# A streaming-encoder layer: branch gates and branch products with tokens on partitions

## The chip, the cores and the metric
The kernel runs on one core of one Trainium2 chip. The metric is the device time of one execution in microseconds (us), as the median of several runs. The core has a matmul engine (TensorE, PE in the profile; its weight loads are listed apart as PEld), VectorE (DVE), ScalarE (ACT), GpSimd (POOL) and SyncE (SP, which here only issues the loads of weights).

## The reference
One layer, 256 tokens, width 2048, float32:

```python
h = rms_norm(x, norm_mix_g)
z = h @ w_in    # qkv 3072 | a 8 | b 8 | gate 1024 | u, v 2048 | attention q, k, v 3072 | gate logits 3 x 2048
branch_a = gated_delta_net(qkv, a, b, gate) @ w_out_a       # 8 heads of 128, the inner width is 1024
u, vb = split(gelu(uv));  vb = layer_norm(vb)
s = einsum('gts,bnsgc->bntgc', ws, vb) + b_spatial          # blocks of 128 tokens, 8 groups
branch_b = (u * s) @ w_out_b
branch_c = stick_breaking_attention(q, k, v) @ w_out_c      # 8 heads of 128
gates = sigmoid(gate_logits)                                # [tokens, 3, 2048]
y = gates[0] * branch_a + gates[1] * branch_b + gates[2] * branch_c
x = x + y @ w_out
x = x + square(relu(rms_norm(x, norm_mlp_g) @ w_ff1)) @ w_ff2   # inner width 8192
```

## The kernel before
**Products in three matmuls.** To reach float32 accuracy, every operand is split into an exact high and low part (`hi` by a copy on ScalarE, `lo` by a subtraction on VectorE, in `split_w`, L151), and a product is the sum of hi x hi, hi x lo and lo x hi. The activations are kept split, as [128, k, 2, 256 tokens] (`actT` holds `hT`, the normalized input, and later `yT`; `aT`, `bT`, `cT` are the branches' inputs). Weights stream in: a `raw` tile of 1 MB (three buffers), which is four *pieces* of 128 x 512 numbers. Both forms of product work piece by piece; a piece is 128 inputs x 512 columns of weights, or 256 inputs x 256 columns, for all 256 tokens:

- `gemm_T` (L193) gives the product transposed, columns on partitions. The weights are stationary; the activations move. For each 128 x 128 block of weights one matmul moves 512 columns (both halves of the activations against `hi`) and one moves 256 (the high half against `lo`): 8 matmuls in a piece. In the trace these are `g<-hT,hi` (512) and `g<-hT,lo` (256), the moving tile first.
- `gemm` (L158) gives the product with tokens on partitions. The activations are stationary and 512 columns of weights move: for each of the two token tiles hi, lo, hi, which are 6 matmuls in a piece, in the trace `g<-hi,hT` and `g<-lo,hT`.

In `gemm_T` the right half of the sum stands in other columns of PSUM, so its reader adds two halves (`add_halves`, L223: a ScalarE copy and a VectorE addition).

**Order of work.** The matmul engine runs in program order; the other engines' order is laid out by a scheduler. `push` (L139) holds the matmuls of a piece back until 4 later pieces have been split (`LA = 4`). Work that is not a streamed product (DeltaNet, normalizations, attention, spatial mixing) consists of generators in the queue `side`; after each piece `pump(1)` runs the first of them to its next `yield`. So between two pieces there may be one step of background work, and `rest(n)` leaves n pieces free so that the other engines can finish what the next step needs.

**Stages.** Decay, gate and qkv projections with DeltaNet behind them (0 to 239 us); the gates of column group 0 (`gate_block(0, br)`, L814) as filling work behind the second DeltaNet half; v, then u of the spatial gating (L885 to L904); attention projections (L1030 to L1032); the gates of group 1 (L1037) as filling behind the attention; the gates of groups 2 and 3 (L1080); the branches' products (`branch_group`, L1046); the output projection; the MLP in four quarters. A column group is 512 of the 2048 columns. All gates and branch products use `gemm_T`, two calls of 256 columns for a group, so `y` is made transposed, as the output projection wants it. A gate's blocks are put into a [128, 4, 256] tile with `scaled_T` (two halves added, times 1 / rms along the free axis) and go through the sigmoid at once or, for groups 0 and 1, later in `early_gates`. At the first block of v, `open_mid` (L822) drains the background queue, releases DeltaNet's tiles and loads the spatial weights `wsT` and `bsp`; the mixing (`gmlp_mix`, L857) is put into the queue when the last block of u is done.

Of the kernel before, what the change touches and what calls it, by code (L numbers as in the profile page):

```python
# [9 lines left out]
F32 = mybir.dt.float32  # L10
# [10 lines left out]
def tile_hybrid_trunk(  # L21
# [48 lines left out]
    # ------------------------------------------------ background work queue  # L70
# [22 lines left out]
    # ------------------------------------------------ constants  # L93
# [7 lines left out]
    # the tensor engine is clocked up only under work: give it some while the first loads run  # L101
# [16 lines left out]
    def split_T(dst, k0, nk, pt, scale=None):  # L118
        """dst[:, k0:k0+nk] = the exact high and low parts of the (scaled) psum tile pt [P, nk, 256]"""
# [14 lines left out]
    # ------------------------------------------------ streamed products  # L134
    # Weights are split into exact high and low parts LA pieces ahead of the products that use them.
# [22 lines left out]
    def gemm(lhs, w, b, done, before=None, rate=0):  # L158
        """done([psum of token tile t]) gets act times block b of w, tokens on partitions"""
# [33 lines left out]
    def gemm_T(act, w, b, done, g0=0, ng=None, rate=0):  # L193
        """done([psum of 128 columns each]) gets (act times block b of w)^T, its low-part half on the right"""
# [71 lines left out]
    W_AG = (352, 344, 344)  # L266
    sgp_ctx = ExitStack()
# [9 lines left out]
    def row_norms():  # L277
        """1 / rms of x's rows, along the free axis (rb) and on partitions (r1); then they scale the first product"""
# [41 lines left out]
    # ------------------------------------------------ more constants  # L320
# [19 lines left out]
    # ------------------------------------------------ branch inputs, transposed  # L340
# [4 lines left out]
    # ================================================ gated DeltaNet  # L345
    gt0ctx = ExitStack()
    gtp0 = gt0ctx.enter_context(tc.tile_pool(name="gtp0", bufs=3))
# [3 lines left out]
    # lvl[b][s, c] = 1 where s lies in the first and c in the second half of one 2b block, in 64 x 64 blocks  # L351
# [26 lines left out]
    # scratch for moving the 16 x 16 diagonal blocks of a 64 x 64 block onto partitions of their own and back  # L378
# [27 lines left out]
    def gates_ab():  # L406
# [10 lines left out]
        # log1p(e) = 2 artanh(e / (2 + e))  # L417
# [32 lines left out]
    def conv_silu(zt, cb0, dst):  # L450
        """causal convolution along the free axis, and SiLU; zt [P, 4, T] is scaled by the row norms first"""
# [18 lines left out]
    def gdn_half(hf, tiles):  # L470
        """heads 4 hf .. 4 hf + 3, in chunks of 128, as tiles come in"""
# [25 lines left out]
        # decay[s, c] = exp(g_c - g_s) for s <= c  # L497
# [70 lines left out]
        # T = (I + L)^-1 and U = T^T: 16 x 16 blocks by substitution, then doubled to 128  # L568
# [76 lines left out]
        for b in (16, 32):  # L645
# [5 lines left out]
            # the last level takes T's first block only  # L651
# [24 lines left out]
        # u = T (beta v); w^T = (beta e^g k)^T T^T for the second chunk  # L676
# [14 lines left out]
        # the state after the first chunk, and what the second takes from it  # L691
# [16 lines left out]
        # output: o = e^g q S + intra v_new, normalized and gated  # L708
# [42 lines left out]
    def scaled_T(pt, dst):  # L751
        """dst = pt's sum of halves times the rows' 1 / rms"""
        add_halves(dst, pt)
        tt(dst, dst, rb, ALU.mult)

    def gate_block(j, br, pool, rate=0):
        gt = []

        def done(i):
            def f(ps):  # L760
                if i == 0:
# [489 lines left out]
```

## Time and profile before

| | us |
|---|---|
| median of 3 runs (lowest, highest) | 1724.08 (1722.41, 1724.3) |
| span of the profiled execution, first to last instruction | 1722.3 |
| matmul engine busy | 1697.8 |
| VectorE busy | 1186.4 |
| ScalarE busy | 963.9 |
| GpSimd busy | 169.5 |

No time of the profiled execution beside its span is shown; the span is 1.8 us below the median and 0.1 us below the lowest run. Busy time of the matmul engine counts a matmul from its issue to its modelled end, and the next one starts earlier than that; its pace is read from the distance of the starts, not from durations.

### The profile page before, as it was taken

To read this page: it belongs to the slowest core of one execution; us is meant where nothing else is said; L and a number is where in the kernel's file an instruction comes from. 1 tells how busy PE (TensorE), PEld (TensorE's weight loads), DVE (VectorE), ACT (ScalarE), POOL (GpSimd) and SP (SyncE) were. 2 spreads that over 40 slices of the span, in tenths; PEclk is the share of its full clock that TensorE was granted. 3 is DMA by queue.
4 is the path that set the end of the run, shared out by engine and by line. 5 is a ranking of instruction groups with operands and counts; after the bars stand their busy time and mean duration, and the time that the engine had idled before them with its cause. 6 is when DMAs were issued, how large, how long until landed. Compare 5 with 4: busy or idle time off the path is not lost.

```text
span 1722.3 us, 26815 instructions
## 1 busy us (share of the span) xinstructions
PE 1697.8 (99%) x9880; PEld 1480.8 (86%) x9880; DVE 1186.4 (69%) x2174; ACT 963.9 (56%) x1741; POOL 169.5 (10%) x225
## 2 busy tenths in 40 slices
PE   8998999999999999999999999999999999999999
PEld 7887888888888888888888888888888888888887
DVE  8885688466658666666787777666776677567764
ACT  5774576465567665555555555544554455445543
POOL 7134024000001000001222100000000000000000
PEclk9999999999999999999999999999999999999999
DMA  7445355355444455555556555555555555555563
GB/s 244 180 144 166 107 179 190 114 189 193 173 170 172 154 189 178 189 191 177 179 209 226 194 196 186 185 192 196 187 186 190 196 192 182 191 194 191 183 217 119
DMA packets 48211, 313.77 MB, mean 182 GB/s; under 512 B 5600, under 2 KB 7792, under 8 KB 12240
## 3 DMA queue, kind: packets, MB, share of 16 engines
q1 hardware_dynamic: 46224, 306.41, 51.2%
q0 software_dynamic: 1856, 5.65, 1.1%
q8 instruction: 77, 1.26, 0.3%
q14 instruction: 54, 0.44, 0.1%
HBM read 308.62 MB, written 3.42 MB: 181 GB/s over the span
## 4 chain that ended last, share of the span: by engine, by line
PE 90%; DVE 3%; DMA 3%; POOL 2%; issue 1%; ACT 1%; DVEq 0%; POOLq 0%; ACTq 0%
PE g L62 86%; PE pm L62 3%; DVE lo L65 1%; POOL tb L65 1%; POOL pr L65 1%; DMA Tm<-scrT 1%; DMA scrU<-ub 1%; DMA lb<-scrL 1%; DMA scrL<-LT 1%; ACT hi L154 0%; DVE qkT L65 0%; DMA ab_bc<-in_a_dt_dram 0%; ACT hT L239 0%; PE pm L928 0%; DVE qkT L458 0%
## 5 line engine op out<-in xcount | busy, mean ns | idle before, releaser
L65 DVE TENSOR_TENSOR lo<-raw,hi 128x512 fp32r<-128x512 f32 (+2 forms) x1168 | 815.3, 705 | 474.5 <-ACT hi L154 469.6
L154 ACT CAST hi<-raw 128x512 fp32r<-128x512 f32 (+2 forms) x1168 | 708.9, 615 | 613.6 <-PE g L62 559.6
L62 PE MATMUL g<-hT,hi 128*128 128x512 f32 x1280 | 464.1, 405 | 0.0
L62 PE MATMUL g<-hT,lo 128*128 128x256 f32 x1280 | 363.2, 284 | 6.8 <-DVE lo L65 6.8
L62 PE MATMUL g<-h2T,hi 128*128 128x512 f32 x1024 | 355.4, 394 | 0.0
L62 PE MATMUL g<-fT,hi 128*128 128x512 f32 x1024 | 355.2, 394 | 0.0
L62 PEld LDWEIGHTS g<-hT,hi 128*128 128x128 f32 x1280 | 243.8, 190 | 58.2
L62 PE MATMUL g<-h2T,lo 128*128 128x256 f32 x1024 | 284.2, 278 | 0.0
L62 PE MATMUL g<-fT,lo 128*128 128x256 f32 x1024 | 284.1, 277 | 0.0
L62 PEld LDWEIGHTS g<-hT,lo 128*128 128x128 f32 x1280 | 245.2, 192 | 9.4 <-DVE lo L65 9.1
L62 PEld LDWEIGHTS g<-fT,hi 128*128 128x128 f32 x1024 | 192.1, 188 | 44.4
L62 PEld LDWEIGHTS g<-h2T,hi 128*128 128x128 f32 x1024 | 192.1, 188 | 44.4
L62 PE MATMUL g<-hi,hT 128*128 128x512 f32 (+2 forms) x704 | 216.5, 379 | 2.8 <-ACT hT L239 1.9
L62 PEld LDWEIGHTS g<-h2T,lo 128*128 128x128 f32 x1024 | 192.4, 188 | 0.0
L62 PEld LDWEIGHTS g<-fT,lo 128*128 128x128 f32 x1024 | 192.4, 188 | 0.0
L62 PEld LDWEIGHTS g<-hi,hT 128*128 128x128 f32 x704 | 130.5, 189 | 23.4 <-ACT hT L239 2.1
L62 PE MATMUL g<-lo,hT 128*128 128x512 f32 (+2 forms) x352 | 131.6, 374 | 1.4 <-DVE lo L65 1.4
L62 PE MATMUL g<-yT,hi 128*128 128x512 f32 x256 | 88.8, 391 | 0.0
L225 ACT COPY half<-g 128x256 f32<-128x256 f32 x192 | 70.4, 369 | 22.8 <-PE g L62 14.7
L62 PEld LDWEIGHTS g<-lo,hT 128*128 128x128 f32 x352 | 66.8, 190 | 11.4 <-DVE lo L65 2.0
L62 PE MATMUL g<-yT,lo 128*128 128x256 f32 x256 | 71.8, 281 | 0.0
L65 DVE TENSOR_TENSOR x<-x,g 128x256 f32<-128x256 f32 x160 | 57.2, 415 | 9.0 <-PE g L62 6.4
(299 smaller groups left out, 1455.6 us busy)
## 6 DMA issues: line engine op xcount, KB each, us to landing
raw<-in_w_ff_dram SPq DMA_DIRECT2D x128, 1024.0 KB, 4.8
raw<-in_w_gl_dram SPq DMA_DIRECT2D x48, 1024.0 KB, 4.8
raw<-in_w_qkv_dram SPq DMA_DIRECT2D x24, 1024.0 KB, 4.9
raw<-in_w_sba_dram SPq DMA_DIRECT2D x24, 1024.0 KB, 4.8
raw<-in_w_out_dram SPq DMA_DIRECT2D x16, 1024.0 KB, 4.8
raw<-in_w_v_dram SPq DMA_DIRECT2D x8, 1024.0 KB, 4.7
raw<-in_w_u_dram SPq DMA_DIRECT2D x8, 1024.0 KB, 4.8
raw<-in_w_out_a_dram SPq DMA_DIRECT2D x8, 1024.0 KB, 4.8
```

Source lines behind the costliest of these rows:

```text
L62: nc.tensor.matmul(out, lhsT, rhs, start=start, stop=stop)
L65: (eng or nc.vector).tensor_tensor(out, a, b, op=op)
L154: nc.scalar.copy(hi, rw)
L225: nc.scalar.copy(tmp, pt[:, T : 2 * T])
```

## The change
Three things are done. (1) A third form of product, `gemm_2`, makes two neighbouring blocks of 256 columns at once with tokens on partitions, in the 6 matmuls of `gemm`, from weights that lie in memory as for `gemm_T`; a `raw` tile is filled by two loads of 512 KB. All gates (12 groups of 16 pieces) and all branch products (12 of 8 pieces) use it. A gate is then evacuated by ScalarE straight from PSUM, with 1 / rms as the row scale, and `y` is made with tokens on partitions. (2) `y` is transposed on the matmul engine, 4 times 8 blocks of 128 x 128, in a generator `y_transposed`, and split from PSUM. (3) The filling behind the second DeltaNet half is now u and the first block of v; the gates of group 0 fill behind the attention, and group 1 stands with 2 and 3. `open_mid` moves to the second block of v, with the mixing right behind it. Core of the diff:

```diff
+    def gemm_2(lhs, w, b, done, rate=0):
+        ps = []
+        nk = 8 * w.shape[1]
+        def piece(kc, hi, lo):
+            if kc == 0:
+                ps.extend(gps())
+            st, sp = kc == 0, kc == nk - 1
+            for t in range(NT):
+                mm(ps[t], lhs(kc, 0, t), hi, st, False)
+                mm(ps[t], lhs(kc, 0, t), lo, False, False)
+                mm(ps[t], lhs(kc, 1, t), hi, False, sp)
+            pump(rate)
+            if kc + 1 == nk:
+                done(ps)
+        for g in range(2 * w.shape[1]):
+            raw = wp.tile([P, 2, 4, 256], F32, tag="raw", name="raw")
+            for i in range(2):
+                nc.sync.dma_start(raw[:, i], w[b + i, g // 2, :, 4 * (g % 2) : 4 * (g % 2) + 4])
+            for h in range(4):
+                hi, lo = split_w(raw[:, :, h, :], [P, 2, 256])
+                flat = lambda x: x.rearrange("p b n -> p (b n)")
+                push(lambda kc=4 * g + h, hi=flat(hi), lo=flat(lo): piece(kc, hi, lo))
...
     def gate_block(j, br, pool, rate=0):
...
-        for i in range(2):
-            gemm_T(lambda kc: actT[:, kc], w_gl, 8 * br + 2 * j + i, done(i), rate=rate)
+        def done(ps):
+            gates[j, br] = gt = pool.tile([P, NT, 512], F32, tag="gt", name="gt")
+            for t in range(NT):
+                nc.scalar.activation(gt[:, t], ps[t], AF.Sigmoid if j else AF.Copy, scale=r1[:, t : t + 1])
+        gemm_2(hl, w_gl, 8 * br + 2 * j, done, rate=rate)
...
-    for br in range(3):
-        gate_block(0, br, gtp0, RG)
...
+    for i in range(4):
+        gemm_T(lambda kc: actT[:, kc], w_u, i, u_done(i), rate=RU)
+    gemm(hl, w_v, 0, v_first, rate=RU)
...
+    def v_done(ps):
+        open_mid()
+        for t in range(NT):
+            nc.scalar.activation(mid["vg"][1][:, t], ps[t], AF.Gelu, scale=r1[:, t : t + 1])
+        side.append(gmlp_norm())
+        side.append(gmlp_mix())
...
+    def y_transposed(j, y):
+        yield from rest(3)
+        for t in range(NT):
+            pt = pm512().rearrange("p (c t) -> p c t", c=4)
+            for c in range(4):
+                nc.tensor.transpose(pt[:, c, :], y[:, t, c * P : (c + 1) * P], ident)
+            d = yT[0][:, 4 * j : 4 * j + 4, :, t * P : (t + 1) * P]
+            nc.scalar.copy(d[:, :, 0], pt)
+            tt(d[:, :, 1], pt, d[:, :, 0].bitcast(F32), ALU.subtract)
+            yield
+        ready["y"] += 1
...
+            gemm_2(lhs_of(tl), w, 2 * j, done(br), rate=1)
...
+    def y_act(kc):
+        if kc >= 12 and not fin:
+            while ready["y"] < 4:
+                pump(1)
+            open_out()
+        return yT[0][:, kc]
```

**Order, first place.** On the matmul engine, one piece of the gates, before (`g0` and `g1` are the PSUM tiles, `hT` the activations, `hi` and `lo` the split weights):

```order
L62 MATMUL g0_7893<-hT_101,hi_7927 128x512
L62 MATMUL g0_7893<-hT_101,lo_7928 128x256
L62 MATMUL g1_7894<-hT_101,hi_7927 128x512
L62 MATMUL g1_7894<-hT_101,lo_7928 128x256
L62 MATMUL g0_7893<-hT_101,hi_7927 128x512
L62 MATMUL g0_7893<-hT_101,lo_7928 128x256
L62 MATMUL g1_7894<-hT_101,hi_7927 128x512
L62 MATMUL g1_7894<-hT_101,lo_7928 128x256
```

The same engine and stage now:

```order
L62 MATMUL g0_7290<-hi_7404,hT_101 128x512
L62 MATMUL g0_7290<-lo_7405,hT_101 128x512
L62 MATMUL g0_7290<-hi_7404,hT_101 128x512
L62 MATMUL g1_7291<-hi_7404,hT_101 128x512
L62 MATMUL g1_7291<-lo_7405,hT_101 128x512
L62 MATMUL g1_7291<-hi_7404,hT_101 128x512
```

Eight matmuls of 512 and 256 columns have become six of 512; the moved columns are 3072 either way.

**Order, second place.** On VectorE, what stands ahead of the mixing: before, the statistics of v (`BN_STATS`, `bst`), the reciprocal root and the normalization of `vg`, between splits:

```order
L847 BN_STATS bst_4118<-vg_3927 128x6
L847 BN_STATS bst_4140<-vg_3927 128x6
L849 BN_AGGR mv_4121<-bst_4118 128x2
L65 TENSOR_TENSOR lo_4129<-raw_4102,hi_4128 128x512
L849 BN_AGGR mv_4143<-bst_4140 128x2
L65 TENSOR_TENSOR lo_4151<-raw_4102,hi_4150 128x512
L853 RECIPROCAL rs_4125<-sd_4123 128x1
```

Now, behind the split of the fifth piece of the first attention block:

```order
L65 TENSOR_TENSOR lo_3883<-raw_3880,hi_3882 128x512
L878 BN_STATS bst_3896<-vg0_113 128x6
L878 BN_STATS bst_3896<-vg1_3877 128x6
L65 TENSOR_TENSOR lo_3908<-raw_3880,hi_3907 128x512
L880 BN_AGGR mv_3899<-bst_3896 128x2
L878 BN_STATS bst_3917<-vg0_113 128x6
L878 BN_STATS bst_3917<-vg1_3877 128x6
L65 TENSOR_TENSOR lo_3929<-raw_3880,hi_3928 128x512
L880 BN_AGGR mv_3920<-bst_3917 128x2
L65 TENSOR_TENSOR lo_3939<-raw_3880,hi_3938 128x512
L884 RECIPROCAL rs_3903<-sd_3901 128x1
L65 TENSOR_TENSOR lo_3951<-raw_3948,hi_3950 128x512
```

The normalization (`TENSOR_SCALAR vg0`) is the next row, and the first mixing matmul (`pm_3970<-wsT_3872,vg0_113`) stands on the matmul engine between the sixth and the seventh piece of the attention's q (`hi_3907`, `hi_3928`). Before, 32 pieces of u lay between the normalization and the mixing.

**Order, third place.** On the matmul engine, in the first block of the output projection (`g0`, `g1<-yT`), where the last group of y is transposed (`pm<-ident,y`):

```order
L1074 MATMUL pm_8654<-ident_75,y_8267 128x128 x4
L62 MATMUL g0_8608<-yT_7441,hi_8604 128x512
L62 MATMUL g0_8608<-yT_7441,lo_8605 128x256
L62 MATMUL g1_8609<-yT_7441,hi_8604 128x512
L62 MATMUL g1_8609<-yT_7441,lo_8605 128x256
L62 MATMUL g0_8608<-yT_7441,hi_8604 128x512
L62 MATMUL g0_8608<-yT_7441,lo_8605 128x256
L62 MATMUL g1_8609<-yT_7441,hi_8604 128x512
L62 MATMUL g1_8609<-yT_7441,lo_8605 128x256
L1074 MATMUL pm_8675<-ident_75,y_8267 128x128 x4
```

Before, the same block ran through with no other matmul in it. Four pieces of the block stand ahead of these rows, one piece (`hi_8618`) behind them, and the piece after that (`hi_8630`) is the first that reads the columns made here.

## Rows read from the trace of the kernel before

**Rows 1.** The page: busy time, share of the span and instructions of each engine.
```profile
PE 1697.8 (99%) x9880; PEld 1480.8 (86%) x9880; DVE 1186.4 (69%) x2174; ACT 963.9 (56%) x1741; POOL 169.5 (10%) x225
```

**Rows 2.** The page: chain that ended last, shares of the span.
```profile
PE 90%; DVE 3%; DMA 3%; POOL 2%; issue 1%; ACT 1%; DVEq 0%; POOLq 0%; ACTq 0%
```

**Rows 3.** Waits of the matmul engine: total us, times, longest us.
```profile
PE g L62 <- DVE lo L65: 8.2, 7, 3.4
PE pm L62 <- DMA Tm<-scrT: 7.4, 2, 4.7
```

**Rows 4.** Timeline, matmuls: start us, duration us, engine, line, op, out<-in, count.
```profile
648.53 0.40 PE L62 MATMUL g<-hT,hi 128*128 128x512 f32 x1
...
784.21 0.40 PE L62 MATMUL g<-aT,hi 128*128 128x512 f32 x1
...
918.90 0.39 PE L62 MATMUL g<-yT,hi 128*128 128x512 f32 x1
```

**Rows 5.** Timeline, matmuls of an attention projection, tokens on partitions.
```profile
473.36 0.62 PE L62 MATMUL g<-hi,hT 128*128 128x512 f32 x2
...
478.80 0.62 PE L62 MATMUL g<-hi,hT 128*128 128x512 f32 x2
```

**Rows 6.** Timeline, matmuls of the second block of w_v.
```profile
358.90 0.62 PE L62 MATMUL g<-hi,hT 128*128 128x512 f32 x2
...
361.64 0.62 PE L62 MATMUL g<-hi,hT 128*128 128x512 f32 x2
```

**Rows 7.** Groups of instructions by form: count | busy us, mean ns | idle before.
```profile
L62 PE MATMUL g<-h2T,hi 128*128 128x512 f32 x1024 | 355.4, 394 | 0.0
```

**Rows 8.** Timeline, matmuls around four transposes between two pieces.
```profile
458.82 0.39 PE L62 MATMUL g<-hi,hT 128*128 128x512 f32 x1
459.06 0.60 PE L928 MATMUL pm<-ident,zq 128*128 128x128 f32 x4
...
459.72 0.39 PE L62 MATMUL g<-lo,hT 128*128 128x512 f32 x1
```

**Rows 9.** Timeline, all engines, around the opening of the spatial-gating pools.
```profile
357.57 1.03 PE L741 MATMUL pm<-ident,o 128*128 128x128 f32 x8
...
359.17 0.60 POOL L831 DMA_DIRECT2D wsT<-in_w_spatial_dram  x1 [60.20 <-ACT aT L743]
...
360.92 1.27 ACT L840 ACTIVATE vg<-g,rr 128x512 f32<-128x512 f32 x2
...
365.06 0.52 POOL L832 MEMSET wsT<- 64x512 f32 x1 [4.72 <-DMA wsT<-in_w_spatial_dram]
```

**Rows 10.** Timeline, all engines: the normalization of the v half.
```profile
382.36 1.28 ACT L851 ACT_TABLE_LOAD   x1
...
383.65 0.48 ACT L851 ACTIVATE sd<-mv,eps_t 128x1 f32<-128x1 f32 x2
...
384.18 0.81 DVE L854 TENSOR_SCALAR vg<-vg,mv,rs 128x1024 f32<-128x1024 f32 x1
```

**Rows 11.** The page: the two splits of weights, count | busy us, mean ns | idle before, releaser.
```profile
L65 DVE TENSOR_TENSOR lo<-raw,hi 128x512 fp32r<-128x512 f32 (+2 forms) x1168 | 815.3, 705 | 474.5 <-ACT hi L154 469.6
L154 ACT CAST hi<-raw 128x512 fp32r<-128x512 f32 (+2 forms) x1168 | 708.9, 615 | 613.6 <-PE g L62 559.6
```

**Rows 12.** DMA issues: out<-in, engine, count, KB each, median us to landing.
```profile
raw<-in_w_gl_dram SPq DMA_DIRECT2D x48, 1024.0 KB, 4.8
...
x<-in_xT_dram POOLq DMA_DIRECT2D x4, 512.0 KB, 10.0
...
wsT<-in_w_spatial_dram POOLq DMA_DIRECT2D x1, 512.0 KB, 5.8
```

**Rows 13.** Groups by form: a product of 128x512 on GpSimd.
```profile
L65 POOL TENSOR_TENSOR kb<-kraw,brk 128x512 f32<-128x512 f32 x4 | 4.6, 1146 | 18.7 <-DVE f L65 18.7
```

**Rows 14.** Timeline, matmuls: the wait for a reload in the second DeltaNet half.
```profile
303.47 0.74 PE L62 MATMUL pm<-Tm,CT 64*64 64x64 f32 x18 [2.67 <-DMA Tm<-scrT]
```

**Rows 15.** Windows: us, busy us per engine (instructions), granted clock, DMA share, GB/s.
```profile
305.00:308.30 3.30, 3.30 (x13) 2.82 (x12) 0.67 (x1) 0.85 (x2) 0.00 (x0) 0.50 0.24 102
```

More of the change, by code (lines that the diff above doesn't have):

```diff
@@ L266, in tile_hybrid_trunk @@
     W_AG = (352, 344, 344)
+    fillctx = ExitStack()
+    fillp = fillctx.enter_context(tc.tile_pool(name="fillp", bufs=1, side="right"))
+    ugT = fillp.tile([P, 8, T], F32, name="ugT")
+    vg0 = fillp.tile([P, NT, 512], F32, name="vg0")
     sgp_ctx = ExitStack()
@@ L933, in sba_half @@
         W = 3 * P
+        sp = late["sp"]
         Z = sp.tile([P, 4, W], F32, tag="Z", name="Z")
@@ L1041, in tile_hybrid_trunk @@
     yctx = ExitStack()
-    yp = yctx.enter_context(tc.tile_pool(name="yp", bufs=6))
+    yp = yctx.enter_context(tc.tile_pool(name="yp", bufs=9))
     brs = ((aT, w_out_a), (bT, w_out_b), (cT, w_out_c))
     yT = {}
+    ready = {"y": 0, "h2": 0}
+    def y_transposed(j, y):
+        yield from rest(3)
+        for t in range(NT):
+            pt = pm512().rearrange("p (c t) -> p c t", c=4)
[6 more added lines that the diff above has]
+        ready["y"] += 1
@@ L1046, in branch_group, with done @@
     def branch_group(j):
-        y = yp.tile([P, 4, T], F32, tag="y", name="y", bufs=2)
-        def done(br, i):
+        y = yp.tile([P, NT, 512], F32, tag="y", name="y", bufs=2)
+        def done(br):
             def f(ps):
-                for k in range(2):
-                    c = 2 * i + k
-                    g, yc = gates[j, br][:, c], y[:, c]
-                    s = ev.tile([P, T], F32, tag="sT", name="sT", bufs=2)
-                    add_halves(s, ps[k])
+                for t in range(NT):
+                    g = gates[j, br][:, t]
@@ L1065, in done @@
+                        tt(y[:, t], y[:, t], g, ALU.add, nc.gpsimd)
+                if br == 2:
+                    side.append(y_transposed(j, y))
             return f
         for br, (tl, w) in enumerate(brs):
-            for i in range(2):
-                gemm_T(lambda kc, tl=tl: tl[:, kc], w, 2 * j + i, done(br, i), rate=1)
-    def early_gates():
-        for key in sorted(gates):
-            if key[0] < 2:
-                nc.scalar.activation(gates[key], gates[key], AF.Sigmoid)
-                yield from rest(3)
@@ L1077, in tile_hybrid_trunk @@
-    side.append(early_gates())
-    for j in (2, 3):
+            gemm_2(lhs_of(tl), w, 2 * j, done(br), rate=1)
+    for br in range(3):
+        nc.scalar.activation(gates[0, br], gates[0, br], AF.Sigmoid)
+    for j in (1, 2, 3):
         for br in range(3):
@@ L1087, in tile_hybrid_trunk @@
     fin = {}
-    ready = {"h2": 0}
     def open_out():
@@ L1117, in wo_evac @@
         if i == 0:
-            yield from rest(4)
+            yield from rest(5)
         for k in range(2):
@@ L1132, in wo_evac @@
             yield from second_norm()
-    push(open_out)
+    def y_act(kc):
[4 more added lines that the diff above has]
+        return yT[0][:, kc]
     for i in range(KD // 2):
-        gemm_T(lambda kc: yT[0][:, kc], w_out, i, lambda ps, i=i: side.append(wo_evac(i, ps)), rate=1)
+        gemm_T(y_act, w_out, i, lambda ps, i=i: side.append(wo_evac(i, ps)), rate=1)
     flush()
```

92 lines of the change are left out of this document (33 added, 59 removed).

## The prediction
> **What bounds the kernel now.** I read the page's busy line first [rows 1]: the matmul engine is busy 99% of the span, VectorE 69%, ScalarE 56%, GpSimd 10%. The chain that ended last runs over the matmul engine for 90% [rows 2]. Its two largest waits are 8.2 us for `lo` splits and 7.4 us for a reload of DeltaNet's `Tm` [rows 3]. So the span is the sum of the matmul engine's issue intervals and some 20 us of waits, and an edit counts by what it does to the distance between matmul starts or by a wait that it makes there. The timeline gives that distance; durations, which overlap, do not.
>
> **The pace of the two forms.** The gates of groups 2 and 3 are 96 pieces from 648.53 to 784.21 us, and all branch products 96 pieces from there to 918.90 [rows 4]: 135.68 / 96 = 1.413 us and 134.69 / 96 = 1.403 us for a piece of `gemm_T`. Tokens on partitions is to be seen in an attention projection with the same `hT`: 24 matmuls from 473.36 to 478.80 [rows 5], 0.2267 us each, so 6 x 0.2267 = 1.360 us for a piece. In w_v it is 2.74 / 12 = 0.2283 us [rows 6], 1.370 us a piece. I take 0.2267, from the longer stretch; the other is the slow bound. All moved columns are the same (3072 a piece), so what is saved is a cost of each matmul, or of a 256-column one, beyond its columns: 8 become 6.
>
> Gates: 12 x 16 = 192 pieces x (1.413 - 1.360) = 10.2 us. Branches: 12 x 8 = 96 pieces x (1.403 - 1.360) = 4.1 us. Together -14.4 us; with 1.370 it is 8.3 + 3.2 = -11.5 us. For the fast bound I let a piece gain as much as the gates' in the branches too: 288 x 0.053 = -15.4 us. A `gemm_T` of the MLP, same form but other stage, runs its 512-column matmuls with a mean duration of 394 ns [rows 7], as long as the 0.40 us in the gates [rows 4], so the gates' pace is no oddity of that stage.
>
> The Trainium skill ("TensorE: Matmul & The Clock Gate", section "Back-to-back issue gap") gives N / 2.4 + 2.5 ns for a single warm matmul; by that, an estimate, the same columns in six matmuls instead of eight save 2 x 2.5 = 5 ns a piece, 1.4 us in all, and the sum, with the additions below, would be +3 us. The trace disagrees with the size: 8 matmuls take 1413 ns in the gates [rows 4] where the rule gives 1300, 6 take 1360 [rows 5] where it gives 1295.
>
> **What it adds on the matmul engine.** y is transposed in 8 sets of four 128 x 128. A set of four between two pieces stands in the attention: from the matmul before it to the one behind it 0.90 us, minus 2 x 0.227 would be one set of 0.45 us [rows 8]. 8 x 0.45 = +3.6 us; nothing hides it. The bounds are 8 x 0.227 = 1.8, if four times 128 columns go like one matmul of 512, and 8 x 0.66 = 5.3, from the first transpose's start to the next piece's, 459.06 to 459.72.
>
> **The wait at the mixing.** It stands behind six pieces of attention q now, 32 pieces of u earlier. Let E be the end of the last v block. Before, `open_mid` at such an end (357.57) issued the load of `wsT` at E + 1.6, `vg` was evacuated at E + 3.4 to E + 4.6, and GpSimd's memset, which waits for the load, ended at E + 8.0 [rows 9]. Statistics, root and normalization took 1.28 us of table load, 0.48 us for two roots and 0.81 us for 1024 numbers [rows 10]. ScalarE has three splits of 0.615 us to do between `vg` and the roots [rows 11]: E + 4.6 + 1.85 + 1.28 = E + 7.7, and from root to normalization 0.53 [rows 10], with a VectorE split of 0.7 in between: E + 9.0, and half of 0.81 for the first token tile: E + 9.4. The matmul engine arrives after 8 transposes of `o` (2 sets, 0.9) and 6 x 1.36: E + 9.05. I take a wait of +0.3 us. Behind that matmul the whole engine is queued. It is 0 if the splits are placed behind the roots, and if `wsT` landed as late as the x loads on the same queue, 10.0 us instead of 5.8 [rows 12], the memset would end at E + 12.2 and the wait be 3.2 us.
>
> **The wait in the output projection.** The last group of y has to be transposed and split before the seventh piece of w_out's first block, E' + 9.2 with E' the end of the branches (6 pieces of 1.41 and two sets of 0.45). The last two additions are two products of 0.7 us and two sums which GpSimd may do at 1.15 us each [rows 13]: y is ready at E' + 3.5, well ahead of the transposes (behind four and five pieces, done at E' + 7.9). A copy on ScalarE and a subtraction on VectorE of 512 numbers follow, about 0.62 + 0.70 by the rows of the splits [rows 11]: E' + 9.2, or E' + 10.5 behind one other split each. I take +0.3, bounds 0 and 1.3.
>
> **What goes and costs nothing.** The gates' evacuation lost its halves' copy and addition; with a split pair of 0.615 and 0.705 us in a piece of 1.36 [rows 11], both engines had room, and their work is off the path. I count 0; should the `lo` waits [rows 3] shrink with it, at most -2 us. 96 + 48 weight loads of 512 KB take the place of 72 of 1 MB on SP's queue; the two of a tile go out together, and SP waits only for a free tile.
>
> **The filling behind DeltaNet.** 48 pieces of gates and 16 of v became 32 of u (same `gemm_T`) and 32 of v up to `open_mid`: as many pieces and steps. The one long wait there, 2.67 us at 303.47 for `Tm` [rows 14], is the reload's latency minus the filling ahead of it; six of those pieces become 0.05 us shorter, so the wait grows by +0.3. Bounds: 0, and 1.65 more, for after that wait the granted clock was 0.50, which is the 1.2 GHz level, from 305 to 308.3 us [rows 15]: at most half of these 3.3 us is lost.
>
> Sum: -14.4 + 3.6 + 0.3 + 0.3 + 0.3 = -9.9. The span of 1722.3 becomes 1712.4; the median of the runs stands 1.8 above that span, so I predict 1714.3 us. The likeliest case's own range, with a pace gain of 11.5 to 15.4, transposes of 1.8 to 5.3 and half of the other bounds, is 1711 to 1718.
>
> **Rivals.**
> - *A long wait at the mixing that halves the clock.* The load of `wsT` takes 10.0 us as x's did [rows 12]: +2.9 beyond my 0.3, and the clock drops for a stretch as behind the 2.67 us wait [rows 15]: +1.65. -9.9 + 4.6 = -5.3, thus 1718.8 (1717 to 1722). For: six pieces are thin cover. Against: before, the very load took 5.8. 12%.
> - *The pace belongs to the stage, not to the form* (slower). If 512 columns cost in the gates what they cost there now, 353 x 2 / 3 = 236 ns, as a rate of the stage (weights arriving, splits just in time), then nothing is gained and the additions stay: +4.5, 1728.6 us. It decides from a pace above 0.2324 us per matmul, where 1728 matmuls eat the additions ((10.2 + 4.1 + 1728 x 0.2267 - 4.5) / 1728 = 0.2324). Against: the attention projection has the same activations, the same splits and 0.2267 [rows 5], and no wait of the gates for splits is among the rows beyond 8.2 us in all [rows 3]. For: w_v is slower already. 8%. By the rule of the skill's clock page the gain would be as small, and the end on this side too, about 1727.
> - *The changed filling removes the reload's wait.* With u's evacuations the steps shift so that `Tm` is back in time: -2.67 - 1.65 [rows 14, 15], 1710.0 (1708.5 to 1711.5). 4%; nothing in the order speaks for it.
> - *Loads of 512 KB starve the splits* (slower). Two `raw` tiles of lead are 8 pieces or 10.9 us; a load of 1 MB landed in 4.8 us, one of 512 KB in 5.8 and four in 10.0 [rows 12]. Only if each piece pair waited over 0.1 us would the gain be gone; 2%, 1727 or more.
>
> The Trainium skill ("DMA: Bandwidth & Descriptors", section "Bandwidth") says to batch DMAs to 1 MiB and fits 2.0 us + bytes / 436 GB/s to one; by that 512 KB takes some 3.2 us, an estimate. No run here shows this load at half its size; either figure is within the lead of 10.9 us.
>
> **How the numbers follow.** My forecast has 74%, the rivals 12, 8, 4 and 2. A measurement of this kernel can tell about 0.2% from no change, 3.4 us: faster means below 1720.6, the same up to 1727.5. The forecast, the third rival and two thirds of the first are faster: 74 + 4 + 8 = 86%. The rest of the first is the same, 4%. The second and the last are slower, 10%. The range from 1709 to 1720.6 leaves out those 10%, the slow end of the first rival and half of the third, and 3% of the forecast's own tails, under 20% in all.
>
> **What would show it.** In the changed trace: 9336 matmuls (9880 - 384 - 192 + 32); the gates' pieces at 1.36 us and the branches' 96 at about 1.36 and 3.6 for transposes, where I would be wrong from 1.395 on; a wait at the first `pm<-wsT` below 1 us with a granted clock of 1.0 behind it; no wait of the first output block over 1.3 us; and the `Tm` wait at about 3 us. A gates stage at 1.41 a piece would mean the second rival, a new wait for `raw` the last.

## The result and the profile after

The changed kernel takes 1733.36 us (median of 20 runs, 1721.79 to 1735.68) against 1722.74 us before (20 runs, 1718.07 to 1726.56): ratio 1.0052, 95% interval 1.0042 to 1.0062. It is slower by half a per cent; 1714.3 was predicted. The runs of the changed kernel stand in groups near 1727 (5) and 1734 (13), with one at 1721.8 and one at 1729.5. The profiled execution is one of the first group, with a span of 1725.9 us.

The page's busy line, chain and a group of the MLP (count | busy us, mean ns | idle before), [rows 1, 2 and 7] before: the matmul count is the predicted 9336, yet the engine is busy 6 us longer, and an MLP matmul lasts 399 ns instead of 394.

```profile
PE 1703.9 (99%) x9336; PEld 1460.7 (85%) x9336; DVE 1149.6 (67%) x2000; ACT 939.0 (54%) x1643; POOL 160.5 (9%) x209
...
PE 93%; DVE 3%; DMA 2%; POOL 1%; issue 1%; ACT 1%; SPq 0%; DVEq 0%; ACTq 0%; POOLq 0%
...
L62 PE MATMUL g<-h2T,hi 128*128 128x512 f32 x1024 | 362.2, 399 | 0.0
```

The starts of the stages on the matmul engine (timeline: start us, duration us, engine, line, op, out<-in, count; [rows 4] before), and the first `h2T` of the kernel before, which the rows did not show:

```profile
771.23 0.39 PE L62 MATMUL g<-hi,aT 128*128 128x512 f32 x1
```

```profile
905.97 0.39 PE L62 MATMUL g<-yT,hi 128*128 128x512 f32 x1
```

```profile
997.64 0.40 PE L62 MATMUL g<-h2T,hi 128*128 128x512 f32 x1
```

```profile
1007.65 0.39 PE L62 MATMUL g<-h2T,hi 128*128 128x512 f32 x1
```

The branch products are entered 13.0 us earlier (784.21 to 771.23). They take 134.74 us, as before (134.69). The output projection takes 91.67 us instead of 88.75. From the first `h2T` (the first matmul of the MLP) to the end of the span it is 728.3 us instead of 714.6: +13.6 us in the MLP, **which the change does not touch**. The four together are -13.0 + 0.1 + 2.9 + 13.6 = +3.6, the difference of the spans.

The same stretch of MLP in both kernels (windows: us, busy us of PE, PEld, DVE, ACT, POOL with instructions, granted clock, DMA share, GB/s), before and then after:

```profile
1120.00:1170.00 50.00, 50.00 (x291) 43.76 (x290) 30.48 (x55) 22.41 (x36) 0.00 (x0) 1.00 0.55 190
```

```profile
1120.00:1170.00 50.00, 50.00 (x284) 43.37 (x284) 30.60 (x56) 22.02 (x36) 0.00 (x0) 1.00 0.56 186
```

Granted clock 1.00 in both, no idle time, the same instructions, and in the two compiled programs the MLP's operands (`h2T`, `fT` and the weights' halves `hi` and `lo`) lie at the same addresses; 291 matmuls against 284. In the timeline, six pairs of 512 + 256 columns, before and then after:

```profile
1199.79 0.40 PE L62 MATMUL g<-h2T,hi 128*128 128x512 f32 x1
...
1201.87 0.40 PE L62 MATMUL g<-h2T,hi 128*128 128x512 f32 x1
```

```profile
1199.82 0.40 PE L62 MATMUL g<-h2T,hi 128*128 128x512 f32 x1
...
1201.94 0.40 PE L62 MATMUL g<-h2T,hi 128*128 128x512 f32 x1
```

2.08 / 6 = 0.347 us a pair before, 2.12 / 6 = 0.353 after. w_out and the MLP keep one of the two from end to end, 0.347 before and 0.353 after; in the kernel before, the gates go at 0.353 and the branches at both, block by block, with one block of branch c in between (0.349). The difference is 6.7 ns a pair; 256 pairs of w_out and 2048 of the MLP make 15.4 us.

The new form has the pace that the prediction gave it. The gates (`hT`, 24 matmuls between the rows), then branch b and branch c (15 each):

```profile
600.33 0.62 PE L62 MATMUL g<-hi,hT 128*128 128x512 f32 x2
...
605.77 0.62 PE L62 MATMUL g<-hi,hT 128*128 128x512 f32 x2
```

```profile
783.93 0.62 PE L62 MATMUL g<-hi,bT 128*128 128x512 f32 x2
...
787.33 0.62 PE L62 MATMUL g<-hi,bT 128*128 128x512 f32 x2
```

```profile
794.16 0.63 PE L62 MATMUL g<-hi,cT 128*128 128x512 f32 x2
...
797.66 0.63 PE L62 MATMUL g<-hi,cT 128*128 128x512 f32 x2
```

0.2267 us for the gates and for b, but 0.2333 for c: 192 matmuls x 0.0067 = +1.3 us that were not foreseen. The mixing and the transposes of the output projection have no wait ahead of them; the first piece that reads the transposed columns starts 0.2 us late, at 915.56:

```profile
363.75 1.13 PE L62 MATMUL pm<-wsT,vg 128*128 128x128 f32 x8
```

```profile
911.63 0.60 PE L1074 MATMUL pm<-ident,y 128*128 128x128 f32 x4
```

The wait for `Tm` ([rows 14]) is gone in this execution (the product starts at 302.20), and with it the halved clock of [rows 15]; by those rows that is 2.67 + 1.65 = 4.3 of the 13.0 us. The start of the kernel, on the other hand, is 1.9 us slower (a matmul that began at 238.25 begins at 240.15). With the 10.2 us of the gates this makes 12.6 of the 13.0.

### The profile page after: what moved, and what is told of

Same layout as the page of the kernel before. It is cut to its first block, busy times and chain, and to the rows that moved or that the text cites. A ratio compares the mean times of both kernels' runs of the same rounds, so it can differ in the third digit from the quotient of the medians.

```text
span 1725.9 us, 25392 instructions
## 1 busy us (share of the span) xinstructions
PE 1703.9 (99%) x9336; PEld 1460.7 (85%) x9336; DVE 1149.6 (67%) x2000; ACT 939.0 (54%) x1643; POOL 160.5 (9%) x209
## 4 chain that ended last, share of the span: by engine, by line
PE 93%; DVE 3%; DMA 2%; POOL 1%; issue 1%; ACT 1%; SPq 0%; DVEq 0%; ACTq 0%; POOLq 0%
PE g L62 89%; PE pm L62 3%; DVE lo L65 1%; DVE hT L267 0%; POOL pr L65 0%; DMA Tm<-scrT 0%; POOL tb L65 0%; DMA scrL<-LT 0%; DMA xs<-in_xT_dram 0%; DMA lb<-scrL 0%; DVE qkT L65 0%; DMA scrU<-ub 0%; ACT hi L154 0%; PE pm L946 0%; DVE qkT L486 0%
## 5 line engine op out<-in xcount | busy, mean ns | idle before, releaser
L65 DVE TENSOR_TENSOR lo<-raw,hi 128x512 fp32r<-128x512 f32 (+2 forms) x1168 | 825.5, 713 | 538.9 <-ACT hi L154 531.7
L62 PE MATMUL g<-hi,hT 128*128 128x512 f32 (+2 forms) x1472 | 458.8, 386 | 3.4 <-DVE hT L267 2.2
L62 PEld LDWEIGHTS g<-hi,hT 128*128 128x128 f32 x1472 | 276.0, 189 | 53.9 <-DVE hT L267 3.0
L62 PE MATMUL g<-lo,hT 128*128 128x512 f32 (+2 forms) x736 | 282.1, 383 | 4.2 <-DVE lo L65 4.2
L62 PE MATMUL g<-hT,hi 128*128 128x512 f32 x512 | 188.5, 409 | 0.0
L62 PEld LDWEIGHTS g<-lo,hT 128*128 128x128 f32 x736 | 139.6, 190 | 29.2 <-DVE lo L65 5.5
L62 PE MATMUL g<-hT,lo 128*128 128x256 f32 x512 | 145.7, 285 | 5.4 <-DVE lo L65 5.4
L62 PEld LDWEIGHTS g<-hT,hi 128*128 128x128 f32 x512 | 98.2, 192 | 22.9
L62 PEld LDWEIGHTS g<-hT,lo 128*128 128x128 f32 x512 | 98.7, 193 | 6.9 <-DVE lo L65 6.6
L62 PEld LDWEIGHTS g<-yT,hi 128*128 128x128 f32 x256 | 48.1, 188 | 12.3 <-DVE yT L65 0.4
```

The lines of the kernel that those rows point to most:

```text
L62: nc.tensor.matmul(out, lhsT, rhs, start=start, stop=stop)
L65: (eng or nc.vector).tensor_tensor(out, a, b, op=op)
```

## Experiments

"Pair" is 512 + 256 columns of `gemm_T`. A "stretch" is a run of matmuls on one operand (`yT`, `h2T`, `fT`); an "interruption" is any other matmul in or between stretches, such as transposes or the product of a norm. "Distance" is the start address of an operand minus that of the weights' halves, modulo 256 bytes, in the compiled program; the traces hold no addresses. The letters A to D and S are theories, each told in the expectation that first uses it. Times of a kernel are those of its several executions; "ratio" is to the kernel before, with its 95% interval.

**The changed kernel again.** No edit.

> The changed kernel as it is, another execution. Theory A (locked pace): the matmul engine's stream of 512 + 256 columns in w_out and the MLP runs at one of two paces, 0.347 or 0.353 us a pair, fixed by the moment at which a stretch is entered and then kept; the 2304 pairs of w_out and MLP then cost up to 15.4 us, and another execution can show another mix of the two: a pair is 0.347 or 0.353 in every long stretch and nothing in between, and the time is 1712 to 1735 us. Theory B (the new layout or traffic slows the later stages): w_out and MLP at 0.353 in this execution too, and any other time comes from elsewhere.

Four groups: 1713.6 | 1720.1, 1720.8 | 1726.4 to 1728.3 (3) | 1734.1 to 1734.9 (4); ratio 1.0026 (0.9998 to 1.0054). The profile is of the second group. Its MLP has the fast pace, in the same code:

```profile
1120.00:1170.00 50.00, 50.00 (x290) 43.71 (x289) 29.92 (x53) 22.40 (x36) 0.00 (x0) 1.00 0.56 190
```

and its second half of DeltaNet waits for `Tm`, with a halved clock behind the wait; after it, the same window of the profile of the result's run:

```profile
307.45 1.76 PE L62 MATMUL pm<-Tm,CT 64*64 64x64 f32 x28 [5.00 <-DMA Tm<-scrT]
```

```profile
304.00:312.00 8.00, 4.55 (x36) 3.93 (x37) 0.00 (x0) 0.59 (x1) 0.00 (x0) 0.61 0.68 190
```

```profile
304.00:312.00 8.00, 8.00 (x115) 6.48 (x114) 3.42 (x6) 2.48 (x4) 0.00 (x0) 1.00 0.46 160
```

36 matmuls against 115 in these 8 us, and the branches are entered at 778.77 instead of 771.23. So two separate things can make the groups: the wait with its clock (7.5 us between these two profiles) and the pace of w_out and MLP (0 or 15.4 us). Together they would give 1712, 1720, 1727 and 1735. Two of the four combinations were profiled; the other two are read from the times. The groups are not sharp, since in the profiles of the other kernels the wait lies between none and 5.0 us, and w_out and MLP can differ in pace (below). Theory B falls.

**Small matmuls ahead of each stretch of the MLP.**

```diff
+            if kc0 == 0 and bump:   # ahead of a stretch's first piece; 16, 32, 48, 64, 96, 128, 192, 256
+                mm(pm512()[:, 0:bump], hi[:, 0, 0:P], act(0)[:, 0, 0:bump])
```

> One additional small matmul (16, 32, 48, 64, 96, 128, 192, 256 columns, its result unused) ahead of each of the eight stretches of the MLP (256 pairs each). Theory A: it moves the moment of entry, so some of the eight stretches go to 0.347 us a pair and some stay at 0.353; each that changes is worth 1.7 us, all eight 13.6. Theory B: all eight stay at 0.353, and the time is that of the changed kernel plus under 1 us.

Windows in the second, third, fifth and sixth stretch:

```profile
1100.00:1180.00 80.00, 80.00 (x463) 70.53 (x463) 48.98 (x87) 35.77 (x59) 0.00 (x0) 1.00 0.57 191
1190.00:1270.00 80.00, 80.00 (x463) 70.57 (x462) 58.50 (x114) 44.81 (x86) 0.00 (x0) 1.00 0.56 193
1370.00:1450.00 80.00, 80.00 (x455) 69.43 (x454) 57.93 (x113) 44.23 (x85) 0.00 (x0) 1.00 0.55 186
1460.00:1540.00 80.00, 80.00 (x455) 69.33 (x454) 47.98 (x85) 35.02 (x57) 0.00 (x0) 1.00 0.56 190
```

463 matmuls in 80 us is 0.347 a pair, 455 is 0.353. Five stretches are fast and three (after the bumps of 96, 128 and 192 columns) slow; the pace changed at three of the eight bumps (16, 96 and 256 columns) and nowhere else. The first of these stands at the second norm, where two kernels below change their pace without a bump; at the other stretch borders of the MLP no profile without bumps changes it. 1726.3 us (1720.5 to 1728.4), ratio 1.0013 (1.0000 to 1.0026). An interruption can change the pace; without one it stayed.

**cT 64 bytes lower.** In the kernels above cT starts at 224 within 256 bytes, all other operands and the weights' halves at 160.

```diff
+        padp = ccx.enter_context(tc.tile_pool(name="padp", bufs=1, side="right"))
+        nc.gpsimd.memset(padp.tile([P, 16], F32, name="pad"), 0.0)
         cpool = ccx.enter_context(tc.tile_pool(name="cpool", bufs=1, side="right"))
```

> The tile cT lies 64 bytes lower, so that its offset within 128 bytes is that of aT and bT. Theory A with an address in it: cT's blocks, which alone took 0.2333 us per matmul, go at 0.2267 as those of aT and bT (4 blocks x 48 matmuls x 0.0067 = -1.3 us), and since the output projection is entered from a cT block, w_out and MLP may go to 0.347 (-15.4 us more). If the address does nothing, cT stays at 0.2333.

The branches take 133.4 us instead of 134.7, cT's blocks going at 0.2267 (15 matmuls between these rows):

```profile
795.37 0.62 PE L62 MATMUL g<-hi,cT 128*128 128x512 f32 x2
...
798.77 0.62 PE L62 MATMUL g<-hi,cT 128*128 128x512 f32 x2
```

w_out was slow, the MLP fast from the second norm's interruption on. 1718.5 us (1710.4 to 1732.3), ratio 0.9974 (0.9948 to 1.0000). The address of cT sets the pace of cT's blocks; it does not fix the pace in which w_out is entered.

**All left tiles 32, then 96 bytes higher.** The edit is a small tile ahead of the pool of weights (`cp.tile([P, 1], ...)`, or 17 columns).

> All tiles of the left side (weights, their halves, hT, aT, bT, yT, h2T, fT) lie 32 bytes higher, so that they begin on 64 bytes; cT stays. If the start address within 64 or 128 bytes sets the pace: other figures than 0.2267, 0.347 and 0.353 in every stage, down to 16 columns' time (6.7 ns) less a matmul, which would be 9336 x 6.7 ns = -62 us at most; aT and bT may take cT's 0.2333 (+3 us). If it does not: the two paces as before.

1711.8 us (4 executions, 1710.8 to 1716.3), ratio 0.9937 (0.9923 to 0.9952); w_out and MLP at 0.347, cT (now at distance 32) still at 0.2333. No figure beyond the known ones: beginning on 64 bytes is not in itself faster.

> All left tiles lie 96 bytes higher, so that they begin on 128 bytes; cT stays at 96 beyond 128. Theory A (the pace is locked at entry and only the moment of entry decides): every execution has w_out and the MLP at 0.347 or 0.353 us a pair, in a mix as for the changed kernel (1712, 1720, 1727 or 1735 us). Theory C (the start address decides which pace is entered): as with the 32 bytes, nearly all executions at 0.347, 1711 to 1717 us. The mixing of aT, bT and cT: cT alone at 0.2333 if its own offset of 96 is what counts, all three at 0.2267 if only the difference to the weights' does.

1732.6 us, ratio 1.0040 (1.0011 to 1.0069), eight of ten above 1725, w_out and MLP slow in the profile. Theory C in its plain form falls: starts on 128 bytes are no cure.

**Left tiles 32 higher and cT 32 lower**, all at distance 0 from the weights.

> Left tiles 32 bytes higher and cT 32 bytes lower, so that all begin 64 bytes beyond a multiple of 128. cT's blocks at 0.2267 us per matmul (-1.3 us), 1710 us where the first kernel with 32 bytes had 1711.8. Theory C: all executions at 0.347 in w_out and MLP. Theory A alone: a mix, several of the executions 15 us longer.

1711.8 us (4 executions), ratio 0.9940 (0.9918 to 0.9961). cT at 0.2267. In the profile w_out is slow and the MLP fast, so the slow pace exists at this address too.

**The order of the change with the old form**: `gate_block` and `branch_group` of the kernel before, the rest of the changed kernel.

> The changed order (u and v fill behind DeltaNet, group 0 of the gates behind the attention) with the old form of gates and branch products, no transposes of y. If the prediction's gain of the form is real (-14.4 + 3.6), this kernel lacks it: gates at 0.353 us a pair; with w_out and MLP at 0.347 and the reload's wait as before 1722 us, with no wait 1718, with the long wait 1725, and with w_out and MLP at 0.353 15 us more. If instead the order made the loss: slower than the changed kernel, 1735 or more.

1727.4 us, ratio 1.0022 (1.0010 to 1.0035). In its profile, which has no wait for `Tm` in the second half either, the branches are entered at 782.79, 11.6 us later than in the changed kernel's; 0.5 of that stands already at 241 us, ahead of the gates, so 11.1 us are left for the form in the gates: its gain there is real (10.2 was predicted).

```profile
782.79 0.40 PE L62 MATMUL g<-aT,hi 128*128 128x512 f32 x1
```

By the medians the order alone loses some 4 us against the kernel before, where +0.3 stood in the sum. Eight of the ten executions are at 1726.7 to 1728.6; the two at 1722.6 and 1722.7, one of them the profiled one without the wait, are no slower than the kernel before.

This kernel also separates the order from the form. Its yT, h2T, fT and weights lie where the changed kernel has them, and the work ahead of the branches has the changed order, but w_out and MLP go at 0.347, as before the change:

```profile
1120.00:1170.00 50.00, 50.00 (x291) 43.74 (x290) 29.94 (x53) 22.39 (x36) 0.00 (x0) 1.00 0.55 190
```

None of its times is 15 us above the others. So it is behind the new form in the branches, with its transposes, that most executions took the slow pace; the new order and layout alone did not bring it.

**The kernel before, left tiles 32 bytes higher.**

> The kernel before with the 32 bytes. Theory A: no more than a redrawn pace: the gates (0.353 before) may go to 0.347 (96 pieces x 2 pairs of a branch stage and gates, at most -5 us), w_out and MLP, which were at 0.347, can only keep it or lose 15 us; 1718 to 1738 us. Theory C (64-byte starts give the fast pace): all stretches of gemm_T at 0.347, 1716 to 1720 us.

1718.8 us, ratio 0.9976 (0.9959 to 0.9992). The first blocks of a and b are still at 0.353; cT (distance 32) goes at 0.347 instead of 0.353, and all blocks behind its first with it.

**The MLP's tiles alone by 32, 64 and 96 bytes** (`n` = 8, 16, 24 columns of 4 bytes; h2T and fT are then at distance 32, 64, 96):

```diff
+        fp.tile([P, n], F32, name="pad")
         fin["x1"] = fp.tile([P, KD, T], F32, name="x1")
```

> The changed kernel with the MLP's tiles (h2T, fT, x1) 32 bytes higher; the weights' halves and everything before the MLP stay. Theory D (the distance of the two operands' start addresses within 128 bytes decides the pace: cT at 64 from the weights was slow in both forms, at 32 fast with stationary weights): h2T and fT at 0.347 us a pair in every execution, 2048 x 0.0067 = 13.7 us less than the changed kernel's slow executions, 1713 to 1722 us. Theory A alone (the moment of entry): a mix, most executions 1727 to 1735.

> The same by 64 bytes, the distance at which cT's blocks were slow. Theory D: 0.353 us a pair in h2T and fT in every execution, none below 1725 us. Theory A alone: a mix, some at 0.347.

> The changed kernel with the MLP's tiles 96 bytes higher. If the distance of the operands within 128 bytes is what decides and 32 and 96 are alike (both half a step of 64 off): all executions at 0.347 in h2T and fT, 1714 to 1723 us, as with 32. If only 32 has it: a mix or 0.350, up to 1735.

The same window for 32, 64 and 96:

```profile
1120.00:1170.00 50.00, 50.00 (x290) 44.30 (x290) 30.64 (x56) 22.33 (x36) 0.00 (x0) 1.00 0.56 191
```

```profile
1120.00:1170.00 50.00, 50.00 (x288) 43.78 (x287) 29.67 (x52) 22.28 (x36) 0.00 (x0) 1.00 0.57 190
```

```profile
1120.00:1170.00 50.00, 50.00 (x288) 43.60 (x287) 30.67 (x56) 22.26 (x36) 0.00 (x0) 1.00 0.57 190
```

At 32: 0.347, and all ten executions within 1718.2 and 1722.8 (ratio 0.9985, 0.9975 to 0.9994); the upper groups are gone, in a kernel that differs from the changed one by 32 bytes. At 64 and 96 there are paces in between, 0.349 and 0.350 (288 matmuls each); executions from 1718 to 1736 and 1718 to 1729 (1.0007, 0.9984 to 1.0029; 1.0023, 1.0007 to 1.0040). Not as expected: 64 is not always slow, 96 is not like 32.

**GpSimd's masks out of DeltaNet's pool.** In the changed kernel the matmul engine's start is slower; its wait at 21 us, GpSimd's work beside it, and the clock:

```profile
21.00 0.66 PE L62 MATMUL g<-lo,hT 128*128 128x352 f32 x1 [3.57 <-DVE lo L65]
```

```profile
16.09 2.43 POOL L65 TENSOR_TENSOR sq<-sq,sqc 128x1024 f32<-128x1024 f32 x1
18.49 2.07 POOL L65 TENSOR_TENSOR sqc<-xs 128x1024 f32<-128x1024 f32 x1
20.64 2.52 POOL L65 TENSOR_TENSOR sq<-sq,sqc 128x1024 f32<-128x1024 f32 x1
```

```profile
20.00:28.00 8.00, 6.53 (x21) 5.97 (x22) 8.00 (x13) 2.91 (x6) 3.12 (x3) 0.50 0.47 143
```

The pool of group 0's gate tiles is gone, so DeltaNet's pool lies where the squares of x are, and its masks, which stood between the squares, wait for them. The edit puts the masks into vg0 and the zeros into ugT.

> The masks and zeros that GpSimd makes in the first 30 us lie in vg0 and ugT (not yet in use) instead of DeltaNet's pool, so that they need not wait for the squares of x and stand among them again, as before the change. Theory S (the changed kernel's start loses 4 us because GpSimd's squares now run one behind the other beside VectorE's splits, which wait, and the matmul engine's clock falls behind that wait): no wait of 3.6 us at 17 to 21 us, granted clock 1.0 from 16 to 28 us, the first gemm_T matmul at 28 us instead of 34, and 3 to 4 us less at 50 us. Rival: the start's loss is the order of loads; nothing changes.

```profile
22.87 0.43 PE L62 MATMUL g<-lo,hT 128*128 128x352 f32 x1 [1.67 <-DVE lo L65]
```

```profile
20.00:28.00 8.00, 6.33 (x39) 5.82 (x38) 7.41 (x11) 2.47 (x6) 7.51 (x13) 1.00 0.55 174
```

The wait is 1.67 us, the clock 1.00, and the first `gemm_T` matmul comes 6.7 us earlier; at 50 us only 1.5 us are left of that, from 170 us on 1.0. What makes the wait and its clock is shown; it was worth 1.0 us at the end and not 3 to 4, because the matmul engine then waits another 4.2 us between 30 and 39 us, where the changed kernel has no wait over 0.3. The other 0.9 of the 1.9 us that the start loses is not explained. Times 1711.9 to 1736.1, ratio 1.0031 (1.0000 to 1.0061), spread as the changed kernel's.

**Four more pieces ahead of Tm's use**: `rest(3 if hf else 8)` becomes `rest(7 if hf else 8)`.

> Seven filling pieces instead of three between the last transposes of v and the use of Tm in DeltaNet's second half, 4 x 1.41 = 5.6 us more of cover. If the wait for Tm there (0 or 3 to 5 us by the execution, and 1 to 3 us of halved clock behind it) makes the split of the times by 7 us: that wait is gone and the times fall in two groups (1712 and 1727) instead of four. If the steps that are pushed back have to be caught up at the end of the second v block: up to 4 x 1 us of waits there.

Two groups, 1719.8 to 1722.6 and 1733.4 to 1734.8 (five each; ratio 1.0024, 0.9997 to 1.0050), which fits the wait as the cause of the 7 us. In the profile the wait in front of `Tm` is gone, but the steps that were pushed back wait at the end of v, so the groups are 1720 and 1734 and not 1712 and 1727:

```profile
359.22 1.69 PE L769 MATMUL pm<-ident,o 128*128 128x128 f32 x8 [4.78 <-DVE o L65]
```

**yT, h2T and fT off the weights' offset, in both kernels.** The padding for yT was 128 bytes, so against the intention aT and bT moved to distance 128, and h2T and fT to 160.

```diff
+    act_view = lambda o, nm: actp.tile([P, KD * 2 * T + 32], F32R, tag="actT", name=nm)[:, o : o + KD * 2 * T]...
+    actT = act_view(0, "hT")
...
+    yT[0] = act_view(8, "yT")
```

> The changed kernel with yT, h2T and fT 32 bytes beyond the weights' offset, cT at the weights' offset, and GpSimd's masks in vg0. Theory D: w_out and MLP at 0.347 in every execution, aT, bT, cT at 0.2267, the start 1.2 us shorter: against the changed kernel's fastest group of 1712 another -1.3 - 1.2, so 1709.5 without the wait for Tm in the second half and 1717 with it; median 1709 to 1717, none above 1720.

> The changed kernel with yT, h2T and fT 32 bytes beyond the weights' offset and nothing else. Theory D: 0.347 us a pair in w_out and MLP in every execution, so the two upper groups (1727, 1735) are gone: 1712 and 1720, median 1712 to 1720, 9 us less than the changed kernel's 1728 to 1733. Theory A alone: four groups as before.

> The kernel before with the same 32 bytes. Its w_out and MLP ran at 0.347 already, so nothing changes: 1718 to 1726, median 1722 to 1724. The difference of g2_T32 to it is then the change's worth without the pace: -10 by the prediction, -4 or so if the start, cT's pace and the longer wait for Tm are counted.

All three have w_out and the MLP at 0.347. But aT and bT at distance 128 went at 0.2333 (in the kernel before, at 0.351 a pair). g1: 1719.5 us, ratio 0.9987 (0.9973 to 1.0000); g2: 1721.1, 0.9988 (0.9975 to 1.0001), all within 1713.9 and 1722.2; g3: 1720.6, 0.9987 (0.9975 to 0.9999). (g1 is the one with the masks, g2 the changed kernel, g3 the kernel before.) The upper groups are gone, the medians of g1 and g2 are 2.5 and 1.1 us above the upper ends expected, and between g2 and g3 the change is worth nothing: in their profiles g2 enters the branches only 2.8 us earlier (777.2 against 780.0), and then loses 1.7 us in the branches (136.8 against 135.1) and 1.3 in w_out (90.0 against 88.75). The gates' gain was smaller, because most of g3's gates went at 0.347 where the kernel before had 0.353, and 3.8 us of it were spent by the start (at 240 us) and 1.4 by the longer wait for `Tm` (4.38 against 2.98).

**Every operand at its faster distance**: hT, aT, bT, cT 0, yT, h2T, fT 32 (padding of 256 bytes for yT); once with the masks in vg0, once with all left tiles 32 bytes higher.

> Distances from the weights' halves within 256 bytes: hT, aT, bT, cT 0, yT, h2T, fT 32; masks in vg0. Theory D: aT, bT and cT at 0.2267 us a matmul (branches 133.4 us instead of 134.7), w_out 90.0 us (0.347), MLP 710.6 us in every execution. With the branches entered at 770 us that makes 1709 us, with the longer wait for Tm 1716; median 1709 to 1717, none above 1719.

> The same distances with all left tiles 32 bytes higher, masks where the changed kernel has them. Theory D: as g5_best, 1 us more for the start: 1710 or 1718, median 1710 to 1718, none above 1720. If the address itself counted and not the distance: another pace in some stage.

Both profiles: branches 133.4, w_out 90.0, MLP 710.6 us from its first matmul to the end of its last. g5: 1717.5 us, ratio 0.9961 (0.9946 to 0.9976), 0.5 above the expected median, one execution at 1719.9; its start had another clock drop (granted 0.62 from 36 to 44 us), and it waited 4.41 us for `Tm`. g6: 1711.1 us (1708.4 to 1715.6), as expected; ratio 0.9934 (0.9919 to 0.9950), not to be told from the 0.9937 and 0.9940 of the two kernels with left tiles 32 bytes higher. Its profile has no wait for `Tm` in the second half; the paces of g5 and g6 are the same. g6's busy line:

```profile
PE 1683.9 (99%) x9336; PEld 1461.2 (86%) x9336; DVE 1148.0 (67%) x2001; ACT 937.2 (55%) x1643; POOL 160.7 (9%) x210
```

13.9 us less than in [rows 1], 20.0 less than in the changed kernel with the same instructions.

## Why the prediction was wrong

**What was right.** The pace of the new form (0.2267 us, gates at 1.360 a piece) and with it the gates' gain: 11.1 us between the changed kernel and its order with the old form, 10.2 predicted. Six sets of transposes in the branches (133.38 - 96 x 1.360 = 2.8 us in the kernel with cT moved, 2.7 predicted). The mixing's wait: none, within its bounds. The output projection, less its 1.7 us of pace: +1.2 us, for two sets and a wait of 0.2. The first rival fell with the mixing's wait, the second with the gates' pace, the loads' with the trace: the 512 KB loads of the gates landed in 4.5 us (median of 96).

**The step that failed.** The sum counted only edited work. It has a heading for what is added and one for what goes, but no term for the 2304 pairs of w_out and MLP behind the change: they were put at nothing without a reason. They were entered from the new form and went at the other of two paces, in 19 of the 20 executions by their times (1727 us and more): +15.4 us, more than the whole gain. The rows had the sign of it. The prediction found 1.413 us a piece of `gemm_T` in the gates and 1.403 in the branches and went on with both, each as the price of its stage; 1.413 is the slow pace throughout (4 x 0.353), 1.403 a mix of the two. [Rows 7] said 394 ns for the MLP where single gates matmuls showed 0.40 us; the prediction read this as equal and concluded that "the gates' pace is no oddity of that stage". But 394 and 399 ns are the two paces, and the MLP's piece took 4 x 0.347 = 1.387 us before the change. So a part of the forecast gain was a gain over the slow pace: against 1.387 the new form's 1.360 saves 5.1 us in the 192 gate pieces and not 10.2. A form that shows two paces in one trace asks which of them each unchanged stage will have afterwards.

**The sum, redone.** The profiled execution has a span of 1725.9 us where the sum gave 1712.4, +13.5. Of that, +15.4 is the pace of w_out and MLP, +1.9 the start, +1.3 the pace of cT, and -4.6 the wait for `Tm` (the 4.3 us that went, and the 0.3 that had been added); with -0.3 for the mixing that makes 13.7. That this execution stands at the near end of the changed kernel's times is luck with `Tm`.

**Sizes that were off.** The wait for `Tm`, "+0.3" with bounds of 0 and 1.65, was gone in one execution (-4.3 with its clock) and in another 5.00 us with more clock behind it, 7.5 us between the two. Ahead of the reload stands a store of 64 KB (`scrT<-tb`). It landed 2.83 us after its issue in the first and 5.41 us in the second; in all profiles here it took 2.7 to 2.9 us, with a wait of at most 1.1, or 4.7 to 6.1 us, with a wait of 2.7 to 5.0. Why it lands late was not tried. The third rival, 4%, happened in the profiled execution and was hidden under the pace. cT's 0.2333: +1.3 us. The start, which no step looked at because no edit stands there: +1.9 us from 170 us on against the kernel before, 1.0 of it by the masks' place.

**Slips in the sums.** Six pieces of 1.41 and two sets of 0.45 are E' + 9.4, not 9.2, which only makes the wait there smaller; 1712.4 + 1.8 is 1714.2. The fit of 2.0 us + bytes / 436 GB/s stands in the Trainium skill, "DMA: Bandwidth & Descriptors", under "Anatomy of one DMA — SWDGE (gpsimd) path" and not under "Bandwidth"; the 3.2 us worked out from it for 512 KB is an estimate, and the gates' loads took 4.5.

**What is settled and what not.** Shown is that the loss is the pace: the same code has it or not from one execution to the next, and 32 bytes in front of the MLP's tiles take it away in all ten. Shown is also that the pace depends on the distance of the operands (us per matmul of tokens on partitions, us per pair of `gemm_T`):

| distance | 512 weight columns moving | pair |
|---|---|---|
| 0 | 0.2267 (hT, aT, bT; cT when moved) | 0.347 or 0.353 |
| 32 | 0.2333 (cT) | 0.347 (MLP in three kernels, cT) |
| 64 | 0.2333 (cT) | 0.349 or 0.353 (MLP, cT) |
| 96 | | 0.350 (MLP) |
| 128 | 0.2333 (aT, bT) | 0.351 (aT, bT) |
| 160 | | 0.347 (MLP in three kernels) |
| 224 | 0.2333 (cT) | |

It is the distance and not one address: h2T and fT at the very same addresses (0 within 256) went at 0.353 with the weights at 0 (all left tiles 96 higher) and at 0.350 with them at 160 (the MLP's tiles 96 higher), and aT and bT at distance 0 went at 0.2267 at three different addresses. aT and bT moved by 256 bytes kept 0.2267, moved by 128 they lost it. At distance 0, where both kernels have w_out and the MLP, two paces are possible; an interruption can change them. The kernel before entered the fast one from its `gemm_T` branches (in its profile, and by its times, none of which is above 1728), and so did the changed order with the old form; the changed kernel mostly entered the slow one from the new form. Why the distance counts, and what picks the pace at distance 0, the runs do not show.

The Trainium skill ("TensorE: Matmul & The Clock Gate", section "Back-to-back issue gap") gives N / 2.4 + 2.5 ns for the gap of a single warm matmul, by which 512 columns take 215.8 ns, an estimate. Here 512 columns took 226.7 or 233.3 ns in a stream at a granted clock of 1.00, by the operands' addresses; the measurement decides.

## What to carry to other kernels

Where the matmul engine is busy all the time, read its pace (starts, not durations) in every long stretch, the unchanged ones too; if one form has two paces, work out what it costs if each stretch takes the other. Compare the start addresses of a matmul's operands modulo 256 bytes when tiles or pools move: here a pad of 32 bytes was worth more (13.6 us in the MLP) than the rewriting of the gates (10 to 11 us). And look at several executions: times that stand in groups, here near 1712, 1720, 1727 and 1735, point at separate causes, and each can be looked for by itself.

## What the hardware showed unexpectedly

- One instruction stream at one granted clock (1.00) has several stable paces, 0.347, 0.349, 0.350, 0.351 or 0.353 us a pair by the operands' distance; at distance 0 the same program ran the MLP, 710 to 724 us, at 0.347 in one execution and at 0.353 in another.
- Tokens on partitions, 512 columns: 0.2267 us when both operands have the same offset within 256 bytes, 0.2333 at each other distance seen (32, 64, 128 and 224).
- A single matmul of 96 or of 256 columns between two stretches changed the pace of the next 90 us.
- Removing a pool used far from the start slowed the start: another pool came to lie on tiles that the first stage still used, which cost 1.0 us in the end.
